# The token tiles of the per-layer gate at every third expert instead of at eight in a row

## The chip, the core and the metric

The kernel runs on one core of a Trainium2 chip. The core has a matrix engine (TensorE, PE in the profile), three engines for elementwise work (VectorE or DVE, ScalarE or ACT, GpSimd or POOL), and SyncE (SP), which here only issues transfers. Each engine works through its own list of instructions in order and waits for the others at semaphores. The metric is the device time of one run in microseconds.

## What is computed

A block with attention, a mixture of experts and a per-layer gate, and then a block of two hybrid layers (retention and stick-breaking attention). All of it is fp32. The change touches the experts and the gate of the first block:

```python
h = h + hier_moe(rms_norm(h, g_ffn[i]), w_rg[i], w_re[i], w1[i], w3[i], w2[i])
h = h + rms_norm(p[i] @ w_ple[i], g_ple[i]) * jax.nn.sigmoid(rms_norm(h, g_plg[i]) @ w_plg[i])
# hier_moe, for each block of at most 128 tokens of one expert:
hdn = jax.nn.silu(xb @ w1[e]) * (xb @ w3[e])
return hdn @ w2[e]
```

There are 1024 tokens of width 1024, 32 experts with a hidden width of 512, and p has 256 columns. `p @ w_ple` needs nothing of the experts, so it can be done at any time before the gate.

## The kernel before

**The experts.** `moe` goes through the 32 experts, one block of 128 gathered tokens each. A product in fp32 is made of three in a reduced format: every operand is split into hi and lo, and `expert` issues hi·hi, hi·lo and lo·hi (L877, L878, L879), 128x512 each. One expert has 24 products for w1, 24 for w3 and 24 for w2, each in two halves (c0 and c1) of 12. Around them stand 8 transposes of the gathered rows `xg` (L887), their split into `exh` (ScalarE, L869) and `exl` (VectorE, L871), the Silu `esg` (ScalarE, L904), its product with the w3 result, `ehd` (VectorE, L905), 4 transposes of `ehd` (L910), their split into `ehh` and `ehl` (again L869 and L871), and the copy of the result, `ey` (ScalarE, L919), which GpSimd scatters to memory.

**The weights.** A half of a weight is a raw load of 1 MB (`mraw`, issued by SyncE, L122) into one of seven buffers. ScalarE makes the hi part (`whi` or `mhi`, L113) and VectorE the lo part (`wlo` or `mlo`, L114), in four pieces of 128x512 each. Three pairs of hi and lo buffers go round, so the split of one half needs the pair that was used three halves earlier in the order w1 c1, w3 c1, then w1 c0 and w3 c0 of the next expert, w2 c0, w2 c1.

**The gate's inputs.** `ple_in` returns a function that does one tile of 128 tokens: it loads `px` (L641), transposes it twice (L644), copies it to `pxT` (L646), does four fp32 matmuls against `w_ple` (L651; each stands in the trace as two records), and then for each half a Square with a sum (ScalarE, L652) and a product with `g_ple` (VectorE, L653). `w_ple` lies in the buffer `wraw` until the last tile is done; the first load of the gate's weight `w_plg` waits for that.

**The order.** The loop in `moe` writes the work down expert by expert with generators, so that the first half of expert e+1 stands ahead of the w2 part of expert e, and a gate tile ahead of the w2 part of its expert. This is not yet the order on the engines: the framework's scheduler simulates the program's timeline and decides from it what each engine does next, as far as data and buffers allow.

Of the kernel before, what the change touches and what calls it, by code (L numbers as in the profile page):

```python
# [18 lines left out]
NT = SEQ // 128  # L19
# [16 lines left out]

PLACE = (4, 7, 8)


MOE_RAW, MOE_HL, MOE_DMA, PIECES, PLE = 3, 1, 1, 4, 4  # L40

LATE = 7

# [1 line left out]
class Kernel:  # L45
# [918 lines left out]
    def moe(self, pgp):  # L964
        tc, nc, I = self.tc, self.nc, self.I
        self.y_d = self.dram.tile([2 * SEQ, D], F32, name="y_d")
        NE = 32
        seq = [k for e in range(NE) for k in
               [(e, "w1", 0), (e, "w3", 0)] * (e == 0) + [(e, "w1", 1), (e, "w3", 1)] +
               [(e + 1, "w1", 0), (e + 1, "w3", 0)] * (e + 1 < NE) + [(e, "w2", 0), (e, "w2", 1)]]  # L970
        raws, ws = {}, {}
        n = [0, 0]

        with self.pool(name="mraw", bufs=1) as rw, ExitStack() as xs:

            bufs = [(self.catp, "cat%d" % j) for j in range(4)] + [(rw, "mraw%d" % j) for j in range(MOE_RAW)]
            xr = xs.enter_context(self.pool(name="xr", bufs=1, side="right"))
            order = bufs[:4] + [None] + bufs[4:] + [(xr, "xraw%d" % j) for j in range(4)]
            NF = len(order)

            def fetch(key):
                e, nm, c = key
                j = n[0]
                n[0] += 1
                b = order[j] if j < NF else bufs[(j - NF) % len(bufs)]
                raw = b[0].tile([128, 2048], F32, name="mraw", tag=b[1]) if b else self.w_raw()
                cs = slice(c * 512, c * 512 + 512)
                raws[key] = self.load_raw(raw, I[nm][0, e][:, cs] if nm == "w2" else I[nm][0, e][cs], 4, 512, dma=MOE_DMA)

            def split(key, pieces=PIECES):  # L990
                n[1] += 1
                hl = (self.w_hl() if n[1] % (2 + MOE_HL) in (1, 2) else
                      [mw.tile([128, 2048], F32R, name="m" + t, bufs=MOE_HL) for t in ("hi", "lo")])
                ws[key] = self.split_w(raws.pop(key), hl, pieces)

            def weights(key):
                if key not in ws:
                    if key not in raws:
                        fetch(key)
                    split(key)  # L1000
                return ws.pop(key)


            for key in seq[:NF]:
                fetch(key)
            xp = self.pool(name="mxg", bufs=1)
            xgs = []
            with xp as xp, self.pool(name="mw", bufs=1) as mw:
                for j in range(2):
                    t = xp.tile([128, D], F32, name="xg%d" % j)  # L1010
                    nc.gpsimd.memset(t, 0.0)
                    xgs.append(t)
                    self.gather(t, self.gidx[:, j:j + 1])
                for j in range(2 + MOE_HL):
                    split(seq[j], 4)
                    fetch(seq[NF + j])
                self.gates()
                last = self.last
                with self.banks(tp=3, mm=5), self.pool(name="mx", bufs=1) as wp, ExitStack() as ps:
                    sc = []  # L1020
                    def start(e):

                        if 2 <= e:
                            self.gather(xgs[e % 2], self.gidx[:, e:e + 1])
                        x = self.expert(wp, xgs[e % 2], *[lambda c, name=name: weights((e, name, c)) for name in ("w1", "w3", "w2")],
                                        self.sidx[:, e:e + 1], False, None if e else last)
                        next(x)
                        return x

                    x = start(0)  # L1030
                    next(x)
                    for e in range(NE):

                        if e + 1 < NE:
                            y = start(e + 1)
                        next(x)
                        if e + 1 < NE:
                            next(y)
                        if PLE <= e < PLE + NT:
                            ple_tile(e - PLE)  # L1040
                        s = next(x)
                        x = y
                        for t in sc:
                            tc.declare_no_dep(s.ins, t.ins, reason="rows of other slots")
                        sc.append(s)
                        if e == 1:
                            with self.pool(name="rd", bufs=1) as cp:
                                self.route_more(cp)
                            xs.close()
                            ple = pgp()  # L1050
                            ple_tile = self.ple_in(ps.enter_context(self.pool(name="pl", bufs=1)), ple)
        return ple
# [494 lines left out]
```

## Time and profile before

| | |
|---|---|
| median of 3 runs | 2946.88 us (2945.25 to 2947.84) |
| profiled execution | 2949.21 us |
| its span, first to last instruction | 2947.4 us |
| TensorE busy | 2710.2 us, 92% |
| VectorE busy | 2127.2 us, 72% |
| ScalarE busy | 1760.7 us, 60% |
| GpSimd busy | 718.0 us, 24% |
| mean granted TensorE clock | 0.967 of full speed |

The span counts from the first to the last instruction; the time of an execution is a little longer. Busy shares are means over the whole program, whose stages differ. The expert loop with the tiles lies between about 900 and 1480 us of the span.

### The profile page before, as it was taken

The numbers are of one execution on the slowest core, as the hardware profiler recorded it, in microseconds if no ns is written. First come the engines' busy times: TensorE is split into PE (matmuls) and PEld (weight loads), VectorE is DVE, ScalarE is ACT, GpSimd is POOL, SyncE is SP. The second block draws the span as 40 slices with busy tenths as digits, with TensorE's granted clock in tenths as the row PEclk, the third lists the DMA queues.
The fourth block names the chain that finished last, engine by engine and source line by source line (L and its number), as shares of the span: only waits on it lengthen the run. The fifth ranks groups of instructions, "written<-read, shape, count | busy, mean of one in ns | idle before, by whom it ended". The sixth has DMA issues, their size and how long they took to land. (4 is left out here: it accounts for less than half of the span.)

```text
span 2947.4 us, 49384 instructions
## 1 busy us (share of the span) xinstructions
PE 2710.2 (92%) x17751; PEld 2447.2 (83%) x17751; DVE 2127.2 (72%) x4362; ACT 1760.7 (60%) x3827; POOL 718.0 (24%) x847
## 2 busy tenths in 40 slices
PE   7999889788979999999959799999989899999988
PEld 7998878678968777877749788999889788899888
DVE  6778589676389888999965458899355368898354
ACT  4444467554258878888846357788342367788242
POOL 0343131563001102111024101650123102650132
PEclk9999999889989999999979899999999899999999
DMA  7766432324279989999851333322562342331661
GB/s 237 248 204 204 130 79 69 64 50 141 109 272 328 314 313 355 368 363 367 308 211 70 115 120 96 98 87 75 199 217 73 116 128 88 98 95 65 223 190 72
DMA packets 390010, 512.92 MB, mean 174 GB/s; under 512 B 94948, under 2 KB 236284, under 8 KB 389252
## 3 DMA queue, kind: packets, MB, share of 16 engines
q1 hardware_dynamic: 375364, 480.37, 49.3%
q0 software_dynamic: 14400, 29.38, 3.0%
q8 instruction: 141, 2.31, 0.3%
q14 instruction: 105, 0.86, 0.1%
HBM read 425.71 MB, written 101.97 MB: 179 GB/s over the span
## 5 line engine op out<-in xcount | busy, mean ns | idle before, releaser
L150 PE MATMUL mm<-whi,acth 128*128 128x256 f32 x2816 | 812.0, 288 | 20.5 <-ACT acth L113 5.7
L152 PE MATMUL mm<-whi,actl 128*128 128x256 f32 x2816 | 807.4, 287 | 6.4 <-DVE rsx L100 3.8
L151 PE MATMUL mm<-wlo,acth 128*128 128x256 f32 x2816 | 804.8, 286 | 0.0
L150 PEld LDWEIGHTS mm<-whi,acth 128*128 128x128 f32 x2816 | 543.7, 193 | 31.7 <-ACT acth L113 7.9
L152 PEld LDWEIGHTS mm<-whi,actl 128*128 128x128 f32 x2816 | 542.6, 193 | 11.0 <-DVE rsx L100 4.3
L151 PEld LDWEIGHTS mm<-wlo,acth 128*128 128x128 f32 x2816 | 543.2, 193 | 3.0 <-issue 0.9
L114 DVE TENSOR_TENSOR wlo<-mraw,whi 128x512 fp32r<-128x512 f32 x508 | 316.1, 682 | 46.7 <-ACT whi L113 46.4
L113 ACT ACTIVATE whi<-mraw 128x512 fp32r<-128x512 f32 x508 | 276.1, 628 | 11.5 <-PE mm L879 9.3
L114 DVE TENSOR_TENSOR wlo<-wraw,whi 128x2048 fp32r<-128x2048 f32 (+1 forms) x64 | 145.5, 2278 | 138.9 <-ACT whi L113 129.1
L1198 PE MATMUL mm<-acth,whi 128*128 128x512 f32 x512 | 201.7, 394 | 0.0
L1200 PE MATMUL mm<-acth,wlo 128*128 128x512 f32 x512 | 201.1, 393 | 0.0
L1199 PE MATMUL mm<-actl,whi 128*128 128x512 f32 x512 | 200.5, 392 | 0.0
L113 ACT ACTIVATE whi<-wraw 128x2048 fp32r<-128x2048 f32 (+1 forms) x64 | 117.0, 1833 | 102.0 <-PE mm L152 67.6
L1240 POOL TENSOR_TENSOR cN<-rx,rcos 128x256 f32<-128x256 f32 x64 | 63.4, 990 | 444.2 <-ACT rx L1237 440.4
L114 DVE TENSOR_TENSOR mlo<-mraw,mhi 128x512 fp32r<-128x512 f32 x256 | 160.2, 680 | 2.9 <-ACT mhi L113 1.6
L1373 ACT ACTIVATE sw<-sw 128x128 f32<-128x128 f32 (+2 forms) x192 | 100.8, 528 | 70.5 <-DVE sw L1372 69.5
L113 ACT ACTIVATE mhi<-mraw 128x512 fp32r<-128x512 f32 x256 | 140.6, 631 | 2.9 <-PE mm L879 2.9
L920 POOL DMA_INDIRECT y_d<-ey,sidx x32 | 39.0, 1219 | 373.5 <-ACT ey L919 364.8
L1366 DVE SCALAR_TENSOR_TENSOR sw<-z,sw 128x128 f32<-128x128 f32 (+1 forms) x192 | 103.8, 547 | 30.3 <-ACT sw L1365 29.5
L1386 DVE TENSOR_TENSOR sal<-tp,sah 128x512 fp32r<-128x512 f32 (+1 forms) x192 | 101.8, 546 | 25.4 <-ACT sah L1385 24.8
L1363 ACT ACTIVATE sw<-z 128x128 f32<-128x128 f32 (+1 forms) x192 | 93.3, 491 | 38.2 <-DVE z L1360 38.0
L1200 PEld LDWEIGHTS mm<-acth,wlo 128*128 128x128 f32 x512 | 96.2, 188 | 19.6
(361 smaller groups left out, 6776.0 us busy)
## 6 DMA issues: line engine op xcount, KB each, us to landing
mraw<-in_w_dram SPq DMA_DIRECT2D x191, 1024.0 KB, 9.0
wraw<-in_w_in_dram SPq DMA_DIRECT2D x88, 512.0 KB, 4.8
mw<-in_w_ada_dram SPq DMA_DIRECT2D x32, 768.0 KB, 6.7
wraw<-in_w_out_dram SPq DMA_DIRECT2D x24, 512.0 KB, 5.3
q_d<-qo SPq DMA_DIRECT2D x32, 256.0 KB, 3.2
q<-q_d POOLq DMA_DIRECT2D x32, 256.0 KB, 2.9
h_d<-res SPq DMA_DIRECT2D x16, 512.0 KB, 2.7
sqk<-sq_d SPq DMA_DIRECT2D x32, 256.0 KB, 4.1
```

What stands on the lines that cost most here:

```text
L113: nc.scalar.activation(hi, raw, AF.Copy)
L114: nc.vector.tensor_sub(lo, raw, hi.bitcast(F32))
L150: nc.tensor.matmul(ps[:, :n], ah[:, k, sl], wh[:, k, :n], start=k == 0, stop=False)
L151: nc.tensor.matmul(ps[:, :n], ah[:, k, sl], wl[:, k, :n], start=False, stop=False)
L152: nc.tensor.matmul(ps[:, :n], al[:, k, sl], wh[:, k, :n], start=False, stop=k == kt - 1)
L1198: nc.tensor.matmul(ps, wh[:, k, cs], hh[:, k], start=k == 0, stop=False)
L1199: nc.tensor.matmul(ps, wh[:, k, cs], hl[:, k], start=False, stop=False)
L1200: nc.tensor.matmul(ps, wl[:, k, cs], hh[:, k], start=False, stop=k == 7)
L1363: nc.scalar.activation(a, z, AF.Abs)
L1366: nc.vector.scalar_tensor_tensor(a, z, 0.0, a, op0=OP.max, op1=OP.add)
L1373: nc.scalar.activation(a, a, AF.Exp)
L1386: nc.vector.tensor_sub(al[ts], pv, ah[ts].bitcast(F32))
```

## The change

`PLE` was the first expert with a tile, and the tiles went with experts 4 to 11. Now `PLE` is the list of the experts that have one: 4, 7, 10, 13, 16, 19, 22, 25.

```diff
-MOE_RAW, MOE_HL, MOE_DMA, PIECES, PLE = 3, 1, 1, 4, 4
+MOE_RAW, MOE_HL, MOE_DMA, PIECES = 3, 1, 1, 4
+PLE = range(4, 28, 3)
...
-                        if PLE <= e < PLE + NT:
-                            ple_tile(e - PLE)
+                        if e in PLE:
+                            ple_tile(PLE.index(e))
```

The changed file has one line more ahead of the functions, so a line there has a number higher by one. Every engine has the same instructions as before; their order is another in nearly the whole expert loop, and a little in the gate that follows and at the end of the first retention.

First place, VectorE at experts 20 and 21. A number behind a name tells the tiles apart. Before, `wlo_14698` is w1 c0 of expert 21, `mlo_14722` w3 c0 of expert 21, `wlo_14747` w2 c0 of expert 20, and `ehd_14678` belongs to expert 20:

```order
L114 TENSOR_TENSOR wlo_14698<-mraw_14695,whi_14697 128x512
L905 TENSOR_TENSOR ehd_14678<-mm_14506,esg_14679 128x256 x2
L114 TENSOR_TENSOR wlo_14698<-mraw_14695,whi_14697 128x512 x3
L871 TENSOR_TENSOR exl_14803<-tp_14804,exh_14802 128x512
L871 TENSOR_TENSOR exl_14803<-tp_14811,exh_14802 128x512
L871 TENSOR_TENSOR ehl_14685<-tp_14686,ehh_14684 128x512
L114 TENSOR_TENSOR mlo_14722<-mraw_14719,mhi_14721 128x512 x4
L114 TENSOR_TENSOR wlo_14747<-mraw_14744,whi_14746 128x512 x4
```

After, `wlo_14664` is w1 c0 of expert 21, `mlo_14688` its w3 c0, `wlo_14713` and `wlo_14739` are the two halves of w2 of expert 20, to which `ehd_14644` and `ehl_14651` belong:

```order
L115 TENSOR_TENSOR wlo_14664<-mraw_14661,whi_14663 128x512 x4
L906 TENSOR_TENSOR ehd_14644<-mm_14455,esg_14645 128x256 x2
L115 TENSOR_TENSOR mlo_14688<-mraw_14685,mhi_14687 128x512 x4
L115 TENSOR_TENSOR wlo_14713<-mraw_14710,whi_14712 128x512 x4
L872 TENSOR_TENSOR exl_14769<-tp_14770,exh_14768 128x512
L872 TENSOR_TENSOR exl_14769<-tp_14777,exh_14768 128x512
L115 TENSOR_TENSOR wlo_14739<-mraw_14736,whi_14738 128x512 x3
L872 TENSOR_TENSOR ehl_14651<-tp_14652,ehh_14650 128x512
```

Before, three split pieces and two `exl` stood between `ehd` and `ehl`; now eleven pieces and two `exl` do, and the w1 half is split ahead of `ehd`. On TensorE, between the last w3 product of expert 20 and the first product with `ehl`, stand 26 products and 12 transposes in both orders: before, 4 products of w1 c0 of expert 21, the transposes, 8 more, 12 of w3 c0 and 2 of w2; now 12 of w1 c0 and 1 of w3 c0, the transposes, 11 of w3 c0 and 2 of w2.

Second place, ScalarE at experts 25 and 26, after the change. `whi_15620`, `mhi_15644` and `mhi_15760` are w1 c0, w3 c0 and w1 c1 of expert 26; `whi_15686` and `whi_15712` are the halves of w2 of expert 25; `pxT` and `ple` are the tile's. Here the tile is a new neighbour; before, experts 25 and 26 had the repeating order of expert 20 above, with two `exh` and `ehh` behind w1 c0 and then w3 c0, w2 c0, w2 c1 and w1 c1 without a break:

```order
L905 ACTIVATE esg_15602<-mm_15428 128x256 x2
L114 ACTIVATE mhi_15644<-mraw_15642 128x512 x4
L647 ACTIVATE pxT_15671<-tp_15668 128x256
L870 ACTIVATE exh_15742<-tp_15744 128x512
L870 ACTIVATE ehh_15607<-tp_15609 128x512
L114 ACTIVATE whi_15686<-mraw_15684 128x512 x4
L114 ACTIVATE whi_15712<-mraw_15710 128x512 x4
L653 ACTIVATE ple_11083,pss_11087<-mm_15673 128x512
L870 ACTIVATE exh_15742<-tp_15751 128x512
L114 ACTIVATE mhi_15760<-mraw_15758 128x512 x4
```

The first Square of the tile and the second `exh` now stand between the splits of w2 and the split of the next w1 half. On TensorE, 24 products (12 of w1 c0, 12 of w3 c0), the 14 transposes and two of the tile's four matmuls stand between the end of expert 25's w1 and w3 products and the first product with `mhi_15760`.

Third place, SyncE's issues around the last tiles. Before:

```order
L641 DMA px<-in_p_dram 128x256
L122 DMA mraw<-in_w_dram 128x4x512 x6
L641 DMA px<-in_p_dram 128x256
L122 DMA mraw<-in_w_dram 128x4x512 x8
L122 DMA wraw<-in_w_plg_dram 128x4x256 x2
L122 DMA mraw<-in_w_dram 128x4x512 x111
```

After:

```order
L642 DMA px<-in_p_dram 128x256
L123 DMA mraw<-in_w_dram 128x4x512 x20
L642 DMA px<-in_p_dram 128x256
L123 DMA mraw<-in_w_dram 128x4x512 x21
L123 DMA wraw<-in_w_plg_dram 128x4x256 x2
L123 DMA mraw<-in_w_dram 128x4x512 x26
```

The raw loads between two `px` loads have become about three times as many, and the first `w_plg` load has moved back by 85 raw loads.

## Rows read from the trace of the kernel before

**Rows 1.** Stages of the expert loop: length, busy us (instructions), clock, DMA share, GB/s.

```profile
937.68:1027.34 89.66, 89.66 (x395) 68.94 (x393) 76.57 (x129) 72.66 (x151) 9.67 (x8) 1.00 0.93 328
1027.34:1116.91 89.57, 86.71 (x377) 65.58 (x376) 73.13 (x125) 68.83 (x146) 8.56 (x8) 1.00 0.90 318
1116.91:1227.94 111.03, 108.74 (x511) 89.36 (x512) 101.85 (x175) 94.80 (x186) 22.45 (x12) 1.00 1.00 362
1227.94:1453.00 225.06, 215.84 (x1010) 176.41 (x1009) 205.46 (x349) 188.21 (x372) 22.24 (x22) 1.00 1.00 364
1453.00:1480.24 27.24, 24.64 (x99) 18.51 (x97) 20.69 (x36) 18.58 (x36) 1.95 (x2) 0.94 0.46 169
```

**Rows 2.** TensorE's timeline at experts 19 and 20: start, length, instruction [idle before].

```profile
1264.26 0.39 PE L877 MATMUL mm<-whi,exh 128*128 128x512 f32 x1
...
1265.18 0.38 PE L910 MATMUL tp<-ident,ehd 128*128 128x128 f32 x2
...
1266.41 0.47 PE L878 MATMUL mm<-wlo,exh 128*128 128x512 f32 x1
...
1269.51 0.50 PE L878 MATMUL mm<-mlo,exh 128*128 128x512 f32 x1 [0.77 <-DVE mlo L114]
...
1272.13 0.39 PE L877 MATMUL mm<-whi,ehh 128*128 128x512 f32 x1
...
1283.01 0.39 PE L877 MATMUL mm<-whi,exh 128*128 128x512 f32 x1
```

**Rows 3.** Waits in experts 18 to 29: us in total, times, longest.

```profile
PE mm L878 <- DVE mlo L114: 9.2, 12, 0.8
...
SPq L122 <- DVE wlo L114: 123.8, 48, 4.5
SPq L122 <- DVE mlo L114: 68.3, 24, 3.8
```

**Rows 4.** VectorE's timeline at experts 19 and 20.

```profile
1271.18 4.89 DVE L114 TENSOR_TENSOR wlo<-mraw,whi 128x512 fp32r<-128x512 f32 x8
...
1283.21 0.76 DVE L905 TENSOR_TENSOR ehd<-mm,esg 128x256 f32<-128x256 f32 x2 [0.82 <-PE mm L879]
1283.88 1.32 DVE L114 TENSOR_TENSOR wlo<-mraw,whi 128x512 fp32r<-128x512 f32 x2
```

**Rows 5.** DMA issues in experts 18 to 29: count, size, median us to landing.

```profile
mraw<-in_w_dram SPq DMA_DIRECT2D x72, 1024.0 KB, 9.1
```

**Rows 6.** TensorE's timeline at expert 8, the gate tile.

```profile
1031.22 0.38 PE L644 MATMUL tp<-ident,px 128*128 128x128 f32 x2
...
1034.87 3.59 PE L651 MATMUL mm<-wraw,pxT 128*128 128x512 f32 x8
```

**Rows 7.** TensorE's waits in experts 8 to 11 and 12 to 17.

```profile
PE mm L877 <- ACT whi L113: 2.7, 4, 0.7
...
PE mm L879 <- DVE ehl L871: 1.0, 1, 1.0
```

**Rows 8.** The tile's Square by source line: ns min/median/max, first and last start.

```profile
L652 ACT ACTIVATE ple<-mm x16: 575/597/619, 951.0 to 1105.7; 128x512 f32<-128x512 f32 x16
L652 ACT ACTIVATION_READ_ACCUMULATOR ple<-mm x16: 188/194/231, 951.5 to 1106.2; 128x1 f32 x16
```

**Rows 9.** ScalarE's timeline at expert 20.

```profile
1288.31 4.28 ACT L113 ACTIVATE whi<-mraw 128x512 fp32r<-128x512 f32 x8
...
1299.22 0.66 ACT L904 ACTIVATE esg<-mm 128x256 f32<-128x256 f32 x2 [2.47 <-PE mm L879]
```

**Rows 10.** TensorE's timeline: two waits outside the experts.

```profile
1818.57 0.66 PE L1382 MATMUL tp<-ident,sw 128*128 128x128 f32 x4 [1.91 <-DVE sal L1386]
...
2815.15 0.66 PE L1426 MATMUL tp<-ident,rq 128*128 128x128 f32 x4 [1.87 <-ACT Tq L1428]
```

**Rows 11.** The stretches behind them, columns as in the first group.

```profile
1820.79:1824.21 3.42, 3.42 (x17) 3.42 (x18) 3.42 (x4) 3.42 (x9) 0.00 (x0) 0.50 0.25 86
...
2815.15:2822.00 6.85, 6.85 (x61) 6.78 (x62) 2.87 (x6) 3.72 (x6) 4.66 (x3) 1.00 0.92 262
```

## The prediction

> **What bounds the kernel now.** I read the stage table first [rows 1]. It cuts the expert loop at the end of an expert's last output copy: experts 4 to 7 and 8 to 11, which carry a gate tile each, 12 to 17, 18 to 29, and the last two. TensorE is busy for 90 to 100% of every stretch but the last, so the loop is bound by TensorE and what remains to gain or lose is its waits. The timeline of TensorE inside one plain expert [rows 2] gives the price of its work. From the first w2 product at 1272.13 to the product at 1283.01 lie 48 products: (1283.01 - 1272.13) / 48 = 0.2267 us each. An expert has 72, which is 16.32 us, and its 12 transposes take 1266.41 - 1265.18 = 1.23 us. That makes 17.55 us. Experts 18 to 29 take 225.06 / 12 = 18.75 us each, so each loses 1.20 us.
>
> The waits [rows 3] say where. In these twelve experts TensorE waits twelve times, 0.8 us at the most by the trace's count, always for VectorE's lo piece `mlo`. VectorE's timeline [rows 4] shows why that piece is late. VectorE works in order, and `ehd` stands in its queue ahead of the splits. `ehd` needs the last w3 product of the running expert, whose slot ends at 1264.26; I call that moment T0. In the next expert the same slot ends at 1283.01 and the two `ehd` start at 1283.21 and give way at 1283.88: T0 + 0.87. Each piece behind them takes about 0.61 us (eight `wlo` pieces in 4.89; `exl` and `ehl` are subtractions of the same shape). The late `mlo` is seventh behind `ehd`: 0.87 + 7 x 0.61 = 5.14, and TensorE started on it at 5.25. Meanwhile TensorE has 13 products and 12 transposes to do: 13 x 0.2267 + 1.23 = 4.18. The wait is 5.25 - 4.18 = 1.07; the other 0.13 of the 1.20 goes to the slower first products after a pause.
>
> The weights are not late. A load is used every 225.06 / 72 = 3.13 us, so each of the seven raw buffers has 21.9 us for a turn, and a load lands 9.1 us after its issue [rows 5]; SyncE stands still for 123.8 + 68.3 of 225 us until VectorE frees a buffer [rows 3]. It is the two split engines behind T0 that hold TensorE.
>
> **What the change costs, part by part.** No instruction is added or removed. A tile costs TensorE 0.22 + 3.59 = 3.81 us [rows 6] whichever expert carries it, so 8 x 3.81 us leave experts 4 to 11 and come back elsewhere: 0 in the sum. The tile's copies and products on ScalarE and VectorE move along. The `px` loads go out three experts apart instead of one; behind the last one, the first `w_plg` load now stands ahead of 26 raw loads and not of 111. It still goes out 26 x 225.06 / 72 = 81 us before the expert loop's last load, so that is 0 too. If the cover failed, a `px` load that came late would cost its landing, below the 9.1 us of a load eight times as large.
>
> What does change is the order of everything behind each expert's T0, since the scheduler lays out the whole loop again. So I compare what TensorE loses to waits, before as measured, after by the same sum.
>
> Before, with a tile expert at 17.55 + 3.81 = 21.36: experts 4 to 7 lose 89.66 - 4 x 21.36 - 18 x 0.2267 = 0.1 (the stretch holds 395 TensorE instructions, 18 more than the 377 of the next); 8 to 11 lose 89.57 - 85.44 = 4.1, with four waits for `whi` [rows 7]; 12 to 17 lose 111.03 - 6 x 17.55 - 7 x 0.2267 = 4.1 (511 instructions instead of 6 x 84 = 504); 18 to 29 lose 225.06 - 210.60 = 14.5. Together 22.8 us.
>
> After, two places in full; the order rows of the section on the change show them.
>
> *Expert 20, VectorE.* Behind `ehd` now stand 4 + 4 split pieces, two `exl`, 3 more pieces and then `ehl`: fourteen. So `ehl` is ready at T0 + 0.87 + 14 x 0.605 = 9.34. In the new TensorE order 26 products and 12 transposes lie between T0 and the first product with `ehl`: 26 x 0.2267 + 1.23 = 7.12. Wait: 2.2 us.
>
> *Experts 25 and 26, ScalarE.* From T0 ScalarE does two `esg` (0.66, begun about 0.2 after T0 as `ehd` is), four pieces of `mhi`, `pxT`, `exh`, `ehh`, eight pieces of `whi`, the tile's Square with its accumulator (0.60 + 0.19 [rows 8]), `exh` and the first piece of the next `mhi`. With 0.53 for a piece or a copy (eight in 4.28 [rows 9]) that is 0.86 + 17 x 0.53 + 0.79 = 10.7, or about 10.4, since consecutive pieces overlap a little. TensorE's cover is 24 products, 14 transposes and half of the tile's matmuls: 5.44 + 1.43 + 1.80 = 8.7. Wait: 1.7. One expert earlier the pair that this expert's last w3 half needs is only given back by the w2 half directly ahead of it: another 1.2.
>
> By the same sum through all experts of the new order I get, in us: expert 6 0.95, 9 1.0, 11 0.5, 14 0.95, 16 0.4, 17 2.0, 18 1.5, 19 1.0, 20 2.2, 21 2.5, 24 0.9, 25 1.2 + 1.7, 26 2.6, 27 2.7, 29 1.5, the rest 0.3. That is 23.9, and about 18 restarts at 0.13 bring 26.2. So experts 4 to 29 change by 26.2 - 22.8 = +3.4 us. The regular 1.2 us per plain expert goes away in half of them, and the irregular order pays it back in fewer, longer waits.
>
> The last two experts (27.24 us now [rows 1]): in expert 31 ScalarE now does both w2 splits before `ehh`, four more pieces at 0.53 with nothing for TensorE to do meanwhile, 1.9 after what the later w2 half gives back; expert 30 loses about 0.5 less: +1.4. Outside the loop only the gate phase and the tail of the first retention are ordered a little differently, with equal counts; I take 0 there, between -3 and +3.
>
> Sum: 2949.2 (the profiled execution, span 2947.4) + 3.4 + 1.4 = 2954.0. That execution lay 2.3 us above the median, so the median of runs comes to 2946.9 + 4.8 = **2951.7 us**.
>
> Bounds of the largest term: if only the waits of 1.5 us and more are real, 16.7 without restarts, the loop changes by -6.1; if each of the 18 is longer by one piece (0.61), by +14.4. With the +1.4 that gives 2942 to 2963 for this case alone.
>
> **The rivals.** *The weight stream holds the plain experts* (faster). For it: in experts 18 to 29 the DMA engines are busy at a share of 1.00 and move 364 GB/s, while the tile experts next to them need 318 to 328 GB/s [rows 1]. If it were so, spreading the tiles' 3.8 us pauses would even the demand out and remove waits: half of 22.8 gives 2935, all 2924. Against it: if the stream held the loop, nearly all seven buffers would be under way at any time and a load would land close to 21.9 us after its issue; it lands after 9.1. The Trainium skill, page "DMA: Bandwidth & Descriptors", section "Where 436 GB/s comes from", puts the limit of loads from HBM at about 358 GB/s per core. By that page the plain experts are at the limit and this rival would hold; the trace's 364 GB/s agrees with the figure, but the landing says that the limit does not yet bite.
>
> *The clock falls* (slower). Five of the new waits are 2.0 us or more; today's longest in the stages of experts 8 to 29 is 1.0 [rows 7], and the granted clock there is 1.00 [rows 1]. Later, in the stick-breaking attention, a wait of 1.91 us that ended at 1818.57 was followed by 3.42 us at a clock of 0.50, the lower of the two levels; another, of 1.87 us, in the second retention, was followed by 1.00 [rows 10, 11]. If all five did as the first, 5 x 3.42 / 2 = 8.6 us more: 2960. The Trainium skill, page "TensorE: Matmul & The Clock Gate", section "HAM oscillation — how this bites in real kernels", tells of idle gaps between stretches of matmuls that bring the clock down again each time. [...]
>
> *ScalarE is behind VectorE at most waits* (slower): each hi piece comes before its lo piece, and I have counted ScalarE's chain as late only in experts 25 and 31. One more piece at each of 18 waits, 0.61 us, gives +11: 2963. It decides as soon as ScalarE frees its queue later than VectorE after T0.
>
> That the change does not do what it says is excluded by the order: the tiles do stand with experts 4, 7, 10 and so on.
>
> **How the numbers follow.** What a measurement can tell from no change is about 0.2%, 5.9 us: from 2941.0 to 2952.8 counts as the same. The old waits replaced by others, as summed: 0.59 (of which faster 0.04, same 0.34, slower 0.21); weight stream 0.17, faster; clock 0.11 and ScalarE 0.13, slower. So faster 0.21, same 0.34, slower 0.45. The range from 2935 to 2965 leaves out the better half of the first rival and the cases in which clock and ScalarE come together, about 2 in 10.
>
> **What would show it.** Right: the twelve waits for `mlo` are gone; waits for `ehl` or a hi piece of 1.7 us and more stand in experts 17, 20, 21 and 25 to 27; experts 12, 13, 15, 22, 23 and 28 run at 17.6 us, or 21.4 where they carry a tile; the loop from expert 4 to the end takes 542.6 + 4.8 us by the same cuts; the granted clock stays 1.00; the stretches outside stay within 3 us. Wrong: TensorE waiting less than 17 us in the loop (VectorE's and ScalarE's queues are then not as late behind T0 as I summed), a clock of 0.50 behind the long waits, or a change of more than 3 us outside the loop, in the retention tail or the gate phase.

## The result and the profile after

The changed kernel takes 2968.80 us in the median of five runs (2959.85 to 2972.20), the kernel before 2946.88 (2944.91 to 2947.84). The ratio is 1.0071, with an interval from 1.0053 to 1.0089: slower, by 21.9 us. The forecast was 2951.7 us, +4.8, with a range up to 2965: the direction was right, though +4.8 lay within the 5.9 us that the prediction itself counted as no change, and the size was four to five times too small. One run in this document, of the kernel before in experiment e10 below, took 4302.62 us at a mean clock of 0.574 and is left out of the ratio there. The profiled execution took 2964.64 us with a span of 2962.9, that is +15.4 against the profiled execution of before.

The stages of the expert loop, cut as before at the end of an expert's last output copy (experts 4 to 7, 8 to 11, 12 to 17, 18 to 29, 30 and 31; the columns are those of [rows 1]), and under them the same table over all of experts 4 to 31:

```profile
936.43:1017.82 81.39, 80.55 (x367) 64.16 (x366) 73.36 (x125) 69.39 (x141) 16.32 (x8) 1.00 0.99 355
1017.82:1104.77 86.95, 85.41 (x397) 68.57 (x396) 76.84 (x131) 70.11 (x141) 12.40 (x9) 1.00 0.98 344
1104.77:1235.64 130.87, 121.49 (x546) 95.06 (x545) 111.44 (x190) 103.85 (x208) 28.38 (x12) 1.00 0.94 329
1235.64:1480.47 244.83, 230.32 (x1032) 180.99 (x1031) 208.32 (x353) 193.28 (x385) 38.04 (x21) 0.99 0.94 329
1480.47:1496.53 16.06, 12.19 (x53) 8.94 (x51) 7.74 (x15) 7.57 (x15) 3.55 (x2) 1.00 0.35 135
...
936.43:1496.53 560.10, 529.96 (x2387) 417.71 (x2385) 477.71 (x810) 444.20 (x888) 98.68 (x52) 1.00 0.93 330
```

ScalarE now gets to these copies later behind an expert's products than before, so that single stages don't compare, only their sum: the five stages of [rows 1] make 542.6 us, these make 560.1. So the loop alone is 17.5 us longer, and everything outside it 2.1 shorter. TensorE is idle for 560.1 - 530.0 = 30.1 us of the loop instead of 17.0; the other 4.4 us are in its busy time, where the first products after a pause run longer and the first part of a pause counts as busy, since a product's record is 0.39 us long while the next one starts after 0.23. VectorE and ScalarE have the same work (477.71 and 444.20 us, before 477.70 and 443.08).

TensorE's waits in the loop, us in total, times and longest, those of more than 1 us in total:

```profile
PE mm L880 <- DVE ehl L872: 9.8, 9, 2.1
PE mm L879 <- DVE mlo L115: 4.8, 7, 1.6
PE mm L878 <- ACT mhi L114: 4.6, 4, 1.8
PE mm L878 <- ACT ehh L870: 4.3, 4, 2.1
PE tp L911 <- DVE ehd L906: 1.7, 2, 1.2
PE mm L878 <- ACT ey L920: 1.3, 1, 1.3
```

Before, the same view gives 16.1 us in 22 waits, more than half of it the regular wait for `mlo` [rows 3]; the rest of it:

```profile
PE mm L877 <- ACT whi L113: 4.1, 6, 0.7
PE mm L879 <- DVE ehl L871: 1.6, 2, 1.0
PE mm L877 <- ACT ehh L869: 0.7, 1, 0.7
PE tp L910 <- DVE ehd L905: 0.5, 1, 0.5
```

Now there are 32 of 29 us, of many kinds and none regular. SyncE still waits for free raw buffers and a load lands 7.6 us after its issue (experts 12 to 26), so the weights are not late. The granted clock falls once in the loop, behind the wait of 2.1 us that ends at 1419.35:

```profile
1420.07:1423.48 3.41, 3.41 (x10) 2.64 (x9) 1.63 (x3) 0.06 (x1) 2.52 (x1) 0.50 0.99 338
```

That costs 3.41 / 2 = 1.7 us. But it fell once in the loop of the kernel before as well, in the last expert, behind waits of 0.5 to 0.7 us:

```profile
1472.63:1476.04 3.41, 3.21 (x8) 2.53 (x9) 2.55 (x5) 0.92 (x2) 0.00 (x0) 0.50 0.85 323
```

So the clock is no part of the 17.5 us. The five runs differ by 12.3 us (those of before by 2.9, but from 2938.60 to 2955.01 when it ran again beside the experiments), and their mean clocks go with them: 0.968 in the fastest, 0.964 in the three slowest. 0.004 of 2967 us is 11.9 us, so TensorE's clock would be enough for the spread. That it is the cause is not shown: a mean given to a thousandth is good to 3 us, and among the runs of before 2949.89 us stands at 0.968 and 2944.50 at 0.964. In which waits it fell in the other runs no trace shows, since only one execution was profiled.

### The profile page after: what moved, and what is told of

Read it like the earlier page. It is cut to its first block, busy times and chain, and to the rows that moved or that the text cites. A ratio compares the mean times of both kernels' runs of the same rounds, so it can differ in the third digit from the quotient of the medians.

```text
span 2962.9 us, 49345 instructions
## 1 busy us (share of the span) xinstructions
PE 2717.7 (92%) x17751; PEld 2450.2 (83%) x17751; DVE 2121.4 (72%) x4362; ACT 1761.9 (59%) x3827; POOL 753.0 (25%) x847
## 5 line engine op out<-in xcount | busy, mean ns | idle before, releaser
L926 POOL DMA_INDIRECT xg<-xf_d,gidx x32 | 53.4, 1668 | 358.4 <-PE tp L888 141.3
L1367 DVE SCALAR_TENSOR_TENSOR sw<-z,sw 128x128 f32<-128x128 f32 (+1 forms) x192 | 103.9, 548 | 29.0 <-ACT sw L1366 28.2
L921 POOL DMA_INDIRECT y_d<-ey,sidx x32 | 58.2, 1820 | 246.7 <-ACT ey L920 223.3
```

Of the source, the lines that this page charges most:

```text
L1367: nc.vector.scalar_tensor_tensor(a, z, 0.0, a, op0=OP.max, op1=OP.add)
```

## The experiments

Four ideas stood against each other. Theory 1: the splits wait for one of the three hi/lo pairs. Theory 2: a tile's copies and products are too much for the split engines at a plain expert. Theory 3: the clock. Theory 4: the order that the scheduler makes of the loop is what costs, not the places of the tiles.

**Four pairs instead of three.** ScalarE's waits had pointed to the pairs. In the changed kernel's loop it waits at a split of `whi` for a TensorE product, which gives back the pair, for 59.6 us:

```profile
ACT whi L114 <- PE mm L880: 59.6, 38, 4.2
```

and in the loop of the kernel before:

```profile
ACT whi L113 <- PE mm L879: 3.7, 5, 1.3
```

The edit makes four pairs, and leaves five raw buffers instead of seven:

```diff
-MOE_RAW, MOE_HL, MOE_DMA, PIECES = 3, 1, 1, 4
+MOE_RAW, MOE_HL, MOE_DMA, PIECES = 1, 2, 1, 4
```

> The changed kernel with four hi/lo pairs instead of three and five raw buffers instead of seven, so that a split waits for the pair of the fourth half before it and not the third. Theory 1 (the splits on ScalarE now wait for a pair that TensorE still holds, 58.9 us of waits in 40 places against 5.9 in 8 before, and what stands behind them on ScalarE and VectorE comes late): these waits fall below 20 us and the kernel comes within 6 us of the kernel before with the same four pairs. Theory 2 (the tile's copies and products load ScalarE and VectorE too much at a plain expert): TensorE's waits stay near 29 us and the difference to the kernel before with four pairs stays at 15 us or more. Theory 3 (TensorE's clock falls after the longer waits): the time follows the mean clock, 3.4 us at half clock after each wait of 2 us or more.

> The kernel before with four hi/lo pairs and five raw buffers; the reference for the run above. Theory 1: little changes, 2935 to 2950 us, since its splits wait for a pair for 5.9 us only. Theory 2 says nothing else. If the raw buffers had been needed it would be slower, with TensorE waiting for splits behind late loads.

Measured: 2968.55 us with the spread tiles, ratio 1.0065 (1.0042 to 1.0088) to the kernel before, and 2964.53, ratio 1.0066 (1.0043 to 1.0089), with the tiles in a row. ScalarE's waits for a pair are gone altogether, and its splits wait for no load, so the two buffers that are missing don't show. But the changed kernel is as slow as it was, and the kernel before has become as slow. TensorE still waits for 27.7 and 25.3 us in the loop. By its letter theory 1 passed in the first run (no waits for a pair, and 4.0 us between the two kernels), but only because the second missed its 2935 to 2950 us. So theory 1 falls: a pair was what ScalarE waited for, not what cost the time. Another number of pairs is also another order, so these two runs don't settle it alone; the run with three pairs and 526 us in the loop further down does. And the tiles' places make no difference that can be told in this setting, although the two are 21 and 17 us slower than the kernel before.

**The scheduler without its timeline.** One argument is changed, for both sets of places:

```diff
-    with tile.TileContext(nc, schedule_with_timeline_sim=True) as tc:
+    with tile.TileContext(nc, schedule_with_timeline_sim=False) as tc:
```

> The changed kernel with the scheduler's reordering by a simulated timeline switched off: every engine goes by the order in which the code is written. It will be much slower as a whole (more than 3000 us). What counts is the difference to the next run. Theory 4 (it is the scheduler's order of the spread tiles that costs, not the tiles' places): within 6 us of the kernel before in program order. Theory 2 (the tile itself costs more at plain experts): 15 us or more slower than it.

> The kernel before in program order, the reference for the run above: more than 3000 us. Theory 4: equal to it within 6 us. Theory 2: at least 15 us faster than it.

Measured: 3228.4 us (spread) and 3233.4 us (row). The whole kernel is slower by 9.5 to 9.7%, but not in the expert loop. From the end of expert 3 to the end of expert 31, spread and then row:

```profile
1101.66:1629.12 527.46, 524.85 (x2395) 417.80 (x2392) 483.77 (x816) 452.43 (x890) 57.90 (x53) 1.00 0.98 353
```

```profile
1103.46:1635.70 532.24, 528.71 (x2395) 417.09 (x2392) 484.86 (x816) 451.50 (x891) 61.15 (x53) 1.00 0.97 350
```

527.5 us against 560.1, 532.2 against 542.6, and TensorE is idle for 3 us. Theory 2 falls, for the tile at a plain expert costs nothing extra here. Theory 3 has fallen already as far as the profiled executions tell, since the clock fell once in the loop of either kernel. The expectations called this the order in which the code is written. That was wrong, as the next runs showed: without its timeline the scheduler still picks from a list of what is ready, and I call its result the list order from here on.

**Holding the engines to the written order.** From expert 4 on, every instruction of the named engines is put behind the one written before it.

```diff
+    @contextmanager
+    def in_order(self, engines):
+        traced = self.nc.cur_bb.bb.instructions
+        n = len(traced)
+        yield
+        prev = {}
+        for i in traced[n:]:
+            if i.engine in engines:
+                if i.engine in prev:
+                    self.tc.add_manual_dep(i, prev[i.engine].name, ...)
+                prev[i.engine] = i
```

> The changed kernel with the scheduler on, but from expert 4 to the end of the loop TensorE, VectorE and ScalarE keep the order in which the loop is written. Theory 4 (the scheduler's order inside the loop is what costs): the loop from the end of expert 3 to the end of expert 31 falls from 560.1 to about 527.5 us, as in program order, and the median to about 2968.8 - 32.6 = 2936 us, faster than both kernels. Theory 2 (the tile at plain experts): it stays above 2960. Theory 3 (clock): no clock below 1.00 in the loop is left, which alone would be worth some 5 us.

> The kernel before with the same pinning. Theory 4: the loop falls from 542.6 to about 532.2 us as in program order, the median to about 2936 us; the eight tiles in a row leave the later experts short of weights (18.3 us an expert from expert 24 on in program order), so it is equal to or up to 5 us slower than the changed kernel with pinning. Theory 2: it is at least 15 us faster than the changed kernel with pinning.

> The changed kernel with TensorE's order alone pinned from expert 4 on; ScalarE and VectorE go as the scheduler then decides. If it is TensorE's order (products of the next expert pulled ahead of the w2 products, which keeps pairs of hi and lo buffers occupied) that costs: near 2936 us. If it is the order on the split engines: near 2965 us.

> The changed kernel with ScalarE's and VectorE's order pinned from expert 4 on, TensorE's left to the scheduler. If it is the order on the split engines that costs: near 2936 us. If it is TensorE's: near 2965 us. Since the scheduler orders all engines in one simulation, pinning one side may bring the other nearly along; then both this run and the one above lie near 2936 us.

Measured: 3211.87, 3204.94, 2990.06 and 3195.47 us. All misses: with all three engines held a plain expert takes 26.5 to 28.2 us, and the loop some 804. The written order puts a split directly ahead of the products that need it, and in the first run TensorE waits for `whi` 62 times:

```profile
PE mm L878 <- ACT whi L114: 75.4, 62, 1.3
```

In the same loop the clock stands at 0.50 in 40 stretches of 3.41 us, which cost 68 us more. This tells nothing of theory 4 except that "program order" had been the wrong name, and that an order alone can cost far more than the change did.

**Holding the engines to the list order.** The program is built twice: first without the timeline, to read off the order of TensorE, VectorE and ScalarE from expert 4 to the end of the loop, and then with the timeline and that order fixed.

```diff
+    nc, names = build(False, None)
+    names = set(names)
+    first = [i.name for f in nc.m.functions for b in f.blocks for i in b.instructions if i.name in names]
+    nc, _ = build(True, first)
```

> The changed kernel with the timeline scheduler on, but from expert 4 to the end of the loop TensorE, VectorE and ScalarE are held to the order that they have in run e3 (the scheduler without the timeline, which is not the order in which the code is written, as e5 showed: pinned to that the loop was far slower). Theory 4 (the order that the timeline scheduler gives the loop is what costs, not the tiles' places): the loop from the end of expert 3 to the end of expert 31 takes about 527.5 us as in e3, against 560.1, and the median comes to 2947 - 15 = 2932 us, faster than both kernels. Theory 2 (tiles at plain experts cost): the loop stays above 550 us.

> The kernel before held to the loop order of run e4 in the same way. Theory 4: the loop takes about 532 us against 542.6 and the median is near 2937 us, about 5 us slower than e9, since from expert 24 on the raw loads land only when they are needed (18.3 us an expert, as in e4). Theory 2: at least 15 us faster than e9.

Measured: 2933.07 us with the spread tiles, ratio 0.9954 (0.9936 to 0.9972) to the kernel before, and 2938.70, ratio 0.9971 (0.9958 to 0.9983), with the row. Both came out within 2 us of what theory 4 gave. The spread tiles with the list order in the loop are faster than both kernels of this study, by 13 and by 36 us. The loops, spread and then row:

```profile
935.33:1461.32 525.99, 522.86 (x2383) 415.71 (x2381) 482.84 (x814) 451.21 (x888) 62.82 (x52) 1.00 0.98 351
```

```profile
937.78:1469.72 531.94, 527.46 (x2383) 414.56 (x2381) 484.23 (x814) 450.29 (x889) 64.95 (x52) 1.00 0.97 347
```

TensorE's waits over the whole loop of the spread version:

```profile
PE tp L912 <- DVE ehd L907: 0.8, 2, 0.5
PE mm L879 <- ACT ehh L871: 0.7, 1, 0.7
PE mm L880 <- DVE wlo L116: 0.5, 2, 0.2
PE mm L880 <- DVE mlo L116: 0.4, 2, 0.2
```

**Other places, the scheduler as it was.** `PLE = range(5, 13)` and `PLE = range(4, 20, 2)`:

> Eight tiles in a row, but at experts 5 to 12 instead of 4 to 11, timeline scheduler as it was. Theory 5 (a row keeps the tiles' disturbance in one stretch and the order then settles into a repeating one, so a row costs little wherever it stands): within 6 us of the kernel before, 2941 to 2953 us. Theory 6 (the order before was a lucky one; any other set of places makes the scheduler fall into a worse one): 2955 us or more.

> The tiles at every second expert from 4 to 18. Theory 5: the disturbance lasts for fifteen experts and not twenty-two, and eleven plain experts in a row remain to settle; about 2955 to 2962 us. Theory 6: anywhere between 2955 and 2975 us, with no relation to the spread.

Measured: 2973.46 us for the row from expert 5 (ratio 1.0089, 1.0071 to 1.0108) and 2975.93 for every second expert (1.0103, 1.0086 to 1.0120). The row is moved by a single expert and loses 28 us. Theory 5 falls, and not because the order never settles: it does, into another repeating order, in which a plain expert takes about 21 us (20.1 to 22.3 from one wait to the next) instead of 18.75 and in ten of eleven times waits 1.6 to 1.8 us for `mlo`. Two of these waits:

```profile
1251.86 0.61 PE L879 MATMUL mm<-mlo,exh 128*128 128x512 f32 x1 [1.79 <-DVE mlo L115]
...
1420.86 0.50 PE L879 MATMUL mm<-mlo,exh 128*128 128x512 f32 x1 [1.80 <-DVE mlo L115]
```

and the stretch behind the first, at half clock (columns of [rows 1]):

```profile
1252.08:1255.49 3.41, 3.41 (x9) 2.63 (x9) 3.41 (x7) 0.38 (x1) 3.41 (x1) 0.50 0.92 350
```

Every second expert ends in the same repeating order, at 20.6 us for each of the last plain experts; its time lies above the 2955 to 2962 us of theory 5 and 0.9 us above the upper end of theory 6. What is left is theory 6: the order before was a good one by chance. Three other sets of places, all slower, speak for it; they are too few to say how rare such an order is.

**Which engine's order, and do the places keep a cost of their own.** Held to the list order: TensorE alone, VectorE and ScalarE alone, and all three with the row from expert 5.

```diff
-ENGINES = (mybir.EngineType.PE, mybir.EngineType.DVE, mybir.EngineType.Activation)
+ENGINES = (mybir.EngineType.PE,)
```

> As e9, but only TensorE is held to the order without the timeline; VectorE and ScalarE are ordered by the timeline scheduler around it. If the cost comes from TensorE's order (products of the next expert between the others, transposes of the gathered rows next to those of ehd): near e9, 2930 to 2940 us, loop near 526 us. If it comes from the queues of VectorE and ScalarE: the loop stays above 545 us and the median above 2950.

> As e9, but only VectorE and ScalarE are held to the order without the timeline, TensorE is ordered by the timeline scheduler around them. If the cost comes from the queues of the split engines: near e9, 2930 to 2940 us. If it comes from TensorE's order: the loop stays above 545 us and the median above 2950.

> The row of eight tiles from expert 5 on, as e11, with the loop held to the order without the timeline on all three engines as in e9. Theory 6 (the timeline scheduler's order is what differs from one set of places to another, and the places themselves hardly matter): 2933 to 2942 us like e10, with a loop near 532 us, although the same places took 2973 us in e11. If the places mattered by themselves, it would keep a good part of the 27 us by which e11 was slower than the kernel before.

Measured: 2966.33 us (loop 556.2), 2963.81 us (loop 560.2), 2934.61 us (loop 530.1). Neither side alone brings anything in time. TensorE's waits fall to 24.0 and 22.8 us, from 29, but the clock stands at 0.50 for 13.6 and 17.1 us of the loop instead of 3.4. My reading, which no run singles out: an order of the split engines is good only for the order in which TensorE asks. And the places that were the slowest row take 2934.61 us as soon as the list order holds, 39 us less, at a ratio of 0.9958 (0.9941 to 0.9975).

## Why the prediction fell short, step by step

**What bounds the loop: right.** TensorE's waits for the split engines, not the weights. Both split engines are busy for the same time as before.

**The chain behind `ehd`: right where I followed it.** Expert 20 was worked out in full: `ehl` 9.34 us behind T0, TensorE's cover 7.12, wait 2.2. In the trace after, VectorE and then TensorE at that place:

```profile
1264.69 0.75 DVE L906 TENSOR_TENSOR ehd<-mm,esg 128x256 f32<-128x256 f32 x2
1265.36 2.49 DVE L115 TENSOR_TENSOR mlo<-mraw,mhi 128x512 fp32r<-128x512 f32 x4
1267.76 2.49 DVE L115 TENSOR_TENSOR wlo<-mraw,whi 128x512 fp32r<-128x512 f32 x4
1270.17 1.28 DVE L872 TENSOR_TENSOR exl<-tp,exh 128x512 fp32r<-128x512 f32 x2
1271.37 1.89 DVE L115 TENSOR_TENSOR wlo<-mraw,whi 128x512 fp32r<-128x512 f32 x3
1273.17 0.69 DVE L872 TENSOR_TENSOR ehl<-tp,ehh 128x512 fp32r<-128x512 f32 x1
...
1271.45 0.40 PE L879 MATMUL mm<-wlo,ehh 128*128 128x512 f32 x1
1273.91 0.50 PE L880 MATMUL mm<-whi,ehl 128*128 128x512 f32 x1 [2.06 <-DVE ehl L872]
```

The wait is 2.06 us by the trace's count; from slot to slot, as the sum counts, it is 1273.91 - 1271.45 - 0.23 = 2.23. The second place came as well: the wait for the first `mhi` piece of w1 c1 of expert 26 was summed to 1.7 and is 1.78 (at 1375.45). Experts 17, 18, 20, 21, 25 to 27 and 31 together: 18.3 us forecast, 16.2 by the trace's count, which comes out about 0.2 to 0.3 lower for each wait than the sum.

**The step that failed: "by the same sum through all experts of the new order".** The mechanism was right, and the term of 26.2 us that it gave was too small. The sum followed each chain from T0 to the first consumer that was plainly late, `ehl` or one hi piece, and took VectorE and ScalarE to be level with TensorE behind it. They are not. One place of ten, at expert 15, which was forecast to run without a wait, VectorE and TensorE:

```profile
1158.07 0.75 DVE L906 TENSOR_TENSOR ehd<-mm,esg 128x256 f32<-128x256 f32 x2
...
1162.94 0.68 DVE L872 TENSOR_TENSOR ehl<-tp,ehh 128x512 fp32r<-128x512 f32 x1
1163.54 4.90 DVE L115 TENSOR_TENSOR wlo<-mraw,whi 128x512 fp32r<-128x512 f32 x8
1168.35 2.49 DVE L115 TENSOR_TENSOR mlo<-mraw,mhi 128x512 fp32r<-128x512 f32 x4
...
1167.10 0.39 PE L878 MATMUL mm<-mhi,exh 128*128 128x512 f32 x1
1169.09 0.50 PE L879 MATMUL mm<-mlo,exh 128*128 128x512 f32 x1 [1.61 <-DVE mlo L115]
```

`ehl` is in time here, and the sum stopped at it with no wait. But behind it VectorE runs on without a gap, through both halves of w2 to the next w1 half, and that `mlo` is eleven microseconds behind `ehd`: TensorE waits 1.61 us. VectorE has little room to catch up: in experts 18 to 29 before, it was busy for 205.46 / 12 = 17.1 us an expert [rows 1], where TensorE's own work is 17.55. Ten waits, 7.1 us by the trace's count, stand where the forecast had none, or 0.4 at expert 16. Six of them, 6.0 us, lie between 1126 and 1191 us: three for `mlo` like this one (3.8 us), the others for the output copy `ey` (1.3), the tile's product `ple` (0.6) and a `whi` (0.3). That each of these comes from a queue still behind was followed only at expert 15. Before, a wait that the trace shows as 0.77 us made an expert 1.20 us longer. With 0.43 more for each, an estimate, the ten come to 7.1 + 10 x 0.43 = 11.4 of the 12.7 us between +4.8 and +17.5 in the loop; the rest is not broken down. Outside the loop the forecast of 0 held within 3 us.

**The bounds.** The upper end of the forecast's own case let every wait that I had found grow by one piece. It left no room for waits that I had not found.

**The rivals.** *The clock* was put at 0.11 and 8.6 us. In the profiled execution it fell once in the loop, 1.7 us, and once before, so it doesn't explain the loop. The median lies 21.9 us higher and not 15.4 because the profiled execution of before lay 2.3 us above its median and that of after 4.2 below; the mean clock of the latter, 0.966 against 0.964 in the median run, would be enough for the 4.2. In the row from expert 5 it is a part of the loss: five stretches of 3.41 us at 0.50 in the loop instead of one, 6.8 us of the 24 by which that loop is longer. There it came down after five of twelve waits of 1.4 to 1.8 us and stayed up after the other seven. The Trainium skill, page "TensorE: Matmul & The Clock Gate", section "HAM oscillation — how this bites in real kernels", tells of gaps that bring the clock down again and again. Its gaps are waits for transfers, longer than any in these two loops, so these loops don't test what it says; they show that the clock can fall behind waits of 0.5 to 2.1 us too, and need not.

*ScalarE behind VectorE* came true in part: ScalarE ended 12 of the 32 waits, 11.9 of the 29 us, and not only in the two experts in which the sum had it late. VectorE ended the other 20.

*The weight stream* was forecast as a reason for a gain. It shows only once the waits are gone. In the list order the row of tiles leaves the later plain experts short. From 1300 to 1440 us, the landing of the loads with the spread tiles and with the row, and ScalarE's wait for loads with the row, of which the spread version has none:

```profile
mraw<-in_w_dram SPq DMA_DIRECT2D x44, 1024.0 KB, 10.9
```

```profile
mraw<-in_w_dram SPq DMA_DIRECT2D x45, 1024.0 KB, 16.5
```

```profile
ACT whi L114 <- DMA mraw<-in_w_dram: 4.8, 6, 2.4
```

A load lands 16.5 us after its issue there and an expert takes 18.3 to 19.5 us, against 17.0 to 17.9 for the plain experts of the spread version (22.3 for those with a tile). Over the loop that is 526.0 us against 531.9 (530.1 with the row from expert 5). So spreading the tiles goes with 4 to 6 us of the loop, less than the 11 to 23 that the rival said, and in the scheduler's own order it is never seen. How much of it is the weights is open. From 1340 us on the row's list order differs too: it has the eight transposes of `xg` in several groups, where the spread version keeps them together. Of the 6.9 us by which the row's eight plain experts behind 1306 us are longer than the 17.8 us of those ahead of them, 2.0 lie ahead of that point and 4.9 behind it.

**What is shown and what is not.** Shown: the order in the loop is the cause, since the same instructions at the same places take 560.1 or 526.0 us by it (e9), and the row from expert 5 takes 566.5 or 530.1 (e11, e15). In keeping with it, one more set of places and the kernel before with a fourth pair also got slower (e12, e2); e2 changes the buffers too. Shown: in the list order the tiles' places as such cost nothing (e3, e9, e15). Argued only: that the ten waits all come from queues that were still behind, and why the scheduler's timeline prefers those orders. That its picture of the durations differs from the chip's is likely, but no run here compares the two.

## What to carry to other kernels

Where a scheduler orders the engines, a change of places is a new draw of the order, and the draw can weigh more than the change: here one expert's shift cost 28 us, the change that was to be judged 22, and in the list order the spread places were 2 to 6 us faster than the two rows. Before judging such a change, fix the order on all engines that take part (not on one), and compare both versions in it; even then the orders of two sets of places need not be alike, as the row's transposes show. And when an order is summed by hand, each chain has to be followed until its engine next stands idle, not until its first late consumer.

## What the runs showed that was not expected

The best order of the loop came from the scheduler with less information: without its timeline TensorE is idle for 3 of 527 us, though the rest of the kernel is about 12% slower with it. What sets that order apart can be read in its VectorE rows around an expert (the version of e9): `ehl` stands three pieces behind `ehd`, and the two `exl` far from both.

```profile
1266.87 0.75 DVE L907 TENSOR_TENSOR ehd<-mm,esg 128x256 f32<-128x256 f32 x2
1267.54 0.68 DVE L116 TENSOR_TENSOR mlo<-mraw,mhi 128x512 fp32r<-128x512 f32 x1
1268.14 1.29 DVE L116 TENSOR_TENSOR wlo<-mraw,whi 128x512 fp32r<-128x512 f32 x2
1269.34 0.69 DVE L873 TENSOR_TENSOR ehl<-tp,ehh 128x512 fp32r<-128x512 f32 x1
...
1279.16 1.29 DVE L873 TENSOR_TENSOR exl<-tp,exh 128x512 fp32r<-128x512 f32 x2 [0.20 <-ACT exh L871]
```

`ehl` is ready 3.2 us after `ehd` begins, where TensorE asks for it some 6 us after (at 1272.85); in the order of the changed kernel it took 9.2. It is the same link that the prediction rests on, with fewer pieces in it.
